# All broadcasts of the group weights issued in one row; the last group's statistics split over two queues

## The chip, the core and the metric

The kernel runs on one core of one Trainium2 chip. The metric is the device time of one execution in microseconds, as the median of several runs. The engines named below are PE (TensorE, the matrix products), DVE (VectorE), ACT (ScalarE), POOL (GpSimd) and SP (SyncE, which only issues transfers). Each engine works through its own instructions in program order and waits on semaphores for the others. ACT, POOL and SP can issue DMA transfers, each into a queue of its own; all queues run on the same 16 DMA engines.

## The reference

One layer of a decoder over 1024 tokens of width 1024, in three sub-layers:

- Sub-layer 1: `a = RMSNorm(x)`; one projection of `a` gives q, k, v of 12 attention heads (three groups of four heads with dilations 1, 4 and 16), a spatial-gating branch, and two sigmoid gates. Attention of each group `g` yields an output `o_g` and a log-denominator `lse_g` per head and token. Per head slot, `y = sum over g of softmax_g(lse_g) * o_g`. Then `merged = gate0 * (y @ w_branch_attn) + gate1 * (y_sgu @ w_branch_sgu)` and `h = x + merged @ w_out`.
- Sub-layer 2: RMSNorm, cross-attention into 256 memory tokens, residual.
- Sub-layer 3: RMSNorm, SwiGLU feed-forward, residual, and a last RMSNorm.

The change touches only the softmax over the three groups: its weights are computed from a maximum and a denominator per head and token, and multiplied onto the attention outputs.

## The kernel before

Everything is float32, each product made of three float32r products (high by high, high by low, low by high), so an operand exists as a pair: `wh`/`wl` for weights, `yAh`/`yAl` for the combined attention output. The large projections use a Strassen-Winograd scheme (lines 383 to 426). The work of sub-layer 1 is staged: projections, then spatial gating, then the product with `w_branch_sgu` (`branch_sgu`, PSUM tiles `psb`, 16 tiles of 12 matmuls), then the product with `w_branch_attn` (`branch_attn`, PSUM tiles `psa`, 16 tiles of 6 matmuls), then the output projection (`seven`, line 1165, PSUM tiles `psx` and `psy`). PSUM has eight banks, handed out in turn (`pp`, line 110); the pool for larger SBUF tiles (`heap`) has 20 buffers.

Attention runs as small pieces that are threaded in between the products of the other branches. The class `Order` (line 37) walks through the main program and lets a piece go on when its time in the plan has come; the tile framework then orders each engine's instructions and sets the waits. What follows the attention of a group is one such piece, `stats(g)`: PE turns the columns of maxima (`nmx`) and denominators (`den`) into rows, DVE copies them to `stT` (line 970), a transfer writes them to DRAM (`sc_d`, line 974, one for each `w_`: 0 is the maxima, 1 the denominators), and four loads for each `w_`, one per head (line 977), bring them back in the layout of `comb`, with 16 partitions per head (`stat`). POOL copies both parts into `comb` (line 981).

When the three groups are through, the piece `combine` works out the weights in `comb` (lines 988 to 999: DVE with one Exp on ACT), writes them to DRAM (`wt_d`, line 1000), and then, for each pair of heads `pr` and each group `g`, loads a tile `wbc` (line 1006): each head's row of 1024 weights is broadcast to 64 partitions, the first head of the pair by ACT's queue and the second by POOL's, 256 KB each. DVE multiplies `oT[g, pr]` by `wbc` (line 1007), adds the groups (lines 1008, 1009) and splits the sum into `yAh` (by ACT, line 137) and `yAl` (by DVE, line 140). `branch_attn` needs the `yAh` and `yAl` of both pairs for each of its tiles. In the kernel before, the loads of a pair stand in the program directly ahead of that pair's products.

While this goes on, PE works on `branch_sgu`, and DVE evacuates each `psb` tile by a product with `mg` (line 1033). On POOL's queue, behind the broadcasts, come the loads of the gates `sig` (line 1041, 512 KB each), which take buffers that the combination frees, and then the loads of `h` (line 1207). DVE evacuates `psa` with a product with `sig` (line 1050) and adds the result to `mg` (line 1051).

Of the kernel before, what the change touches and what calls it, by code (L numbers as in the profile page):

```python
# [15 lines left out]
P = 128  # L16
# [69 lines left out]
def tile_hybrid_dilated_attn_sgu_gated_block(  # L86
# [25 lines left out]
    nc = tc.nc  # L112
# [11 lines left out]
    def H(name, dt=F32, shape=(P, 1024)):  # L124
        return heap.tile(list(shape), dt, name=name, tag="h")
# [4 lines left out]
    def W(name, dt=F32, shape=(P, 512)):  # L130
        return wk.tile(list(shape), dt, name=name, tag="w")

    def PS(name="ps", shape=(P, 512)):
        return pp.tile(list(shape), F32, name=name, tag="p")

    def split(src, hi, lo, pin=False, eng=None):
        i = nc.scalar.activation(hi, src, AF.Copy)  # L137
        if pin:
            tc.keep_in_program_order(i)
        (eng or nc.vector).tensor_sub(lo, src, hi.bitcast(F32))  # L140
# [530 lines left out]
    qk, vts, oT = {}, {}, {}  # L671
# [170 lines left out]
    def spawn_attn():  # L842
        its = [(g, pr) for g in range(GROUPS) for pr in range(2)]

        def add(i):
            if i < len(its):
                load_qk(*its[i])
            yield 0.0, 0.0

        for i, (g, pr) in enumerate(its):  # L850
            st = {"n": 0}
            for n, it in enumerate(units(g)):
                order.spawn(attn_it(g, pr, it, st), delay=2.0, key="attn%d" % g)
                if n == 4:
                    order.spawn(add(i + 2), key="load")
            if pr == 1:
                order.spawn(stats(g), key="stats")
        order.spawn(combine(), key="combine")
# [96 lines left out]
    sc_d = dram.tile([GROUPS, 2, HPG, S], F32, name="sc_d")  # L955
    wt_d = dram.tile([GROUPS, HPG, S], F32, name="wt_d")

    def comb(i):
        return consts_["comb"][:64, i * 64:(i + 1) * 64]

    def stats(g):
        while order.busy("attn%d" % g):
            yield 0.0, 1.0
        if g == 0:
            consts_["comb"] = H("comb")
        ps = PS("pst")
        stT = W("stT")
        for w_, t in enumerate((nmx, den)):
            nc.tensor.transpose(ps[:32, w_ * P:(w_ + 1) * P], t[:, g * 32:(g + 1) * 32], ident)
        nc.vector.tensor_copy(stT[:32, :256], ps[:32, :256])  # L970
        d = DIL[g]
        stat = W("stat")
        for w_ in range(2):
            nc.sync.dma_start(sc_d[g, w_].rearrange("h (b q) -> (h b) q", q=P), stT[:32, w_ * P:(w_ + 1) * P])
            src = sc_d[g, w_].rearrange("h (r c i) -> h c r i", r=d, i=64 // d)
            for h in range(HPG):
                nc.sync.dma_start(
                    stat[h * 16:(h + 1) * 16, w_ * 64:(w_ + 1) * 64].rearrange("p (r i) -> p r i", r=d), src[h])
        yield 0.22, 0.0
        for w_ in range(2):  # L980
            nc.gpsimd.tensor_copy(comb(3 * w_ + g).rearrange("p (i r) -> p i r", r=d),
                                  stat[:64, w_ * 64:(w_ + 1) * 64].rearrange("p (r i) -> p i r", r=d))

    def combine():
        while order.busy("stats"):
            yield 0.0, 1.0
        low, tot = comb(6), comb(7)
        nc.vector.tensor_tensor(low, comb(0), comb(1), op=ALU.min)
        nc.vector.tensor_tensor(low, low, comb(2), op=ALU.min)
        for g in range(3):  # L990
            nc.vector.tensor_sub(comb(g), low, comb(g))
        n_, dn_ = [consts_["comb"][:64, i * 192:(i + 1) * 192] for i in range(2)]
        nc.scalar.activation(n_, n_, AF.Exp)
        nc.vector.tensor_mul(dn_, dn_, n_)
        nc.vector.tensor_add(tot, comb(3), comb(4))
        nc.vector.tensor_add(tot, tot, comb(5))
        nc.vector.reciprocal(low, tot)
        for g in range(3):
            nc.vector.tensor_mul(comb(g), comb(g), low)
            nc.scalar.dma_start(wt_d[g].rearrange("h (c i) -> (h c) i", i=64), comb(g))  # L1000
        for pr in range(2):
            for g in range(3):
                t = H("wbc")
                for hh in range(2):
                    src = wt_d[g, 2 * pr + hh:2 * pr + hh + 1, :]
                    (nc.scalar, nc.gpsimd)[hh].dma_start(t[hh * HD:(hh + 1) * HD, :], src.to_broadcast([HD, S]))
                nc.vector.tensor_mul(oT[g, pr], oT[g, pr], t)
            nc.vector.tensor_add(oT[0, pr], oT[0, pr], oT[1, pr])
            nc.vector.tensor_add(oT[0, pr], oT[0, pr], oT[2, pr])
            y = H("yAh", F32R), H("yAl", F32R)  # L1010
            split(oT[0, pr], *y)
            yA.append(y)
            yield 0.0, 0.0
# [82 lines left out]
    h = []  # L1096
# [24 lines left out]
    WPART = ("W11", "W21", "T2", "T1", "W22", "T3", "T4")  # L1121

    def seven(kp, raw, weights, combine, done, tail, after=None, todo=()):


# [4 lines left out]
        def prep(n):  # L1130
            s_, k = steps[n]
            if k % 2 == 0:
                wld[s_] = load([weights[WPART[s_]][k:min(k + 2, kp)].rearrange("k p c -> p k c")])[0]
            hi = whl.tile([P, 1024], F32R, name="wh", tag="hi")
            lo = whl.tile([P, 1024], F32R, name="wl", tag="lo")
            split(raw(s_, k), hi[:, :HALF], lo[:, :HALF])
            split(wld[s_][:, (k % 2) * HALF:(k % 2 + 1) * HALF], hi[:, HALF:], lo[:, HALF:])
            ready[n] = (hi, lo)
            combine(s_, k)
# [507 lines left out]
```

## Time and profile before

| what | value |
|---|---|
| median of 3 runs | 1486.52 us (1485.70 to 1486.54) |
| the profiled execution's own time | 1485.01 us |
| its span | 1483.2 us |
| PE busy | 1445.8 us (97%) |
| DVE busy | 993.5 us (67%) |
| ACT busy | 609.2 us (41%) |
| POOL busy | 143.4 us (10%) |

The span is what the profiler saw between the first and the last instruction; the execution's own time is 1.8 us longer. PE is busy nearly throughout, so what can be changed in the time is to be looked for in the few places in which PE has nothing to do, or runs at the lower clock. A busy PE says nothing of its pace; the granted clock of a stretch (1.00 is 2.4 GHz, 0.50 is 1.2 GHz) and the distance from one matmul's start to the next do.

### The profile page before, as it was taken

To read this page: it belongs to the slowest core of one execution; us is meant where nothing else is said; L and a number is where in the kernel's file an instruction comes from. 1 tells how busy PE (TensorE), PEld (TensorE's weight loads), DVE (VectorE), ACT (ScalarE), POOL (GpSimd) and SP (SyncE) were. 2 spreads that over 40 slices of the span, in tenths; PEclk is the share of its full clock that TensorE was granted. 3 is DMA by queue.
4 is the path that set the end of the run, shared out by engine and by line. 5 is a ranking of instruction groups with operands and counts; after the bars stand their busy time and mean duration, and the time that the engine had idled before them with its cause. 6 is when DMAs were issued, how large, how long until landed. Compare 5 with 4: busy or idle time off the path is not lost.

```text
span 1483.2 us, 19504 instructions
## 1 busy us (share of the span) xinstructions
PE 1445.8 (97%) x7375; PEld 1210.7 (82%) x7375; DVE 993.5 (67%) x1855; ACT 609.2 (41%) x1150; POOL 143.4 (10%) x166
## 2 busy tenths in 40 slices
PE   8999999999998999899999999999999999999997
PEld 8899888888887768687888888888888888888876
DVE  7786555555546855898677896666666663876596
ACT  4245233343335771135456752222222221454463
POOL 5300000000012112100000000110110002200030
PEclk9999999999999999999999999999999999999999
DMA  6224333793379247532211313885874225943342
GB/s 214 65 91 129 115 114 114 208 244 108 108 237 311 85 173 185 161 115 68 72 53 62 114 58 119 213 209 143 219 176 129 80 84 184 377 149 93 107 149 78
DMA packets 162897, 211.78 MB, mean 143 GB/s; under 512 B 9150, under 2 KB 110258, under 8 KB 162676
## 3 DMA queue, kind: packets, MB, share of 16 engines
q1 hardware_dynamic: 134304, 127.09, 27.1%
q0 software_dynamic: 22640, 68.98, 16.8%
q10 hardware_dynamic: 5860, 14.47, 3.0%
q8 instruction: 58, 0.95, 0.3%
q14 instruction: 35, 0.29, 0.1%
HBM read 168.43 MB, written 73.55 MB: 163 GB/s over the span
## 4 chain that ended last, share of the span: by engine, by line
PE 84%; DVE 7%; DMA 5%; ACT 2%; issue 1%; POOL 0%; SPq 0%; ACTq 0%; POOLq 0%; DVEq 0%
PE psb L390 20%; PE psc L390 13%; PE psg L390 13%; PE psx L1165 8%; PE psy L1165 8%; PE psv L170 1%; PE psv L169 1%; PE psv L171 1%; DVE wl L140 1%; DMA wbc<-wt_d 1%; PE psb L469 1%; PE psq L171 1%; PE psq L170 1%; PE psq L169 1%; DVE nq L204 1%
## 5 line engine op out<-in xcount | busy, mean ns | idle before, releaser
L137 ACT ACTIVATE wh<-wst 128x1024 fp32r<-128x1024 f32 (+1 forms) x213 | 178.7, 840 | 348.2 <-PE psg L390 244.3
L140 DVE TENSOR_TENSOR wl<-wst,wh 128x512 fp32r<-128x512 f32 (+1 forms) x209 | 205.1, 983 | 82.2 <-ACT wh L137 82.2
L390 PE MATMUL psg<-A,wh 128*128 128x512 f32 x592 | 182.5, 389 | 0.0
L390 PEld LDWEIGHTS psg<-A,wh 128*128 128x128 f32 x592 | 111.1, 188 | 22.9
L390 PE MATMUL psg<-A,wl 128*128 128x512 f32 x296 | 115.2, 389 | 0.0
L390 PE MATMUL psc<-S,t 128*128 128x512 f32 x444 | 106.6, 389 | 0.0
L390 PEld LDWEIGHTS psc<-S,t 128*128 128x128 f32 x444 | 83.4, 188 | 17.3
L1165 PE MATMUL psx<-wh 128*128 128x512 f32 x240 | 93.9, 393 | 3.1 <-DVE h L1177 3.1
L1165 PE MATMUL psx<-wl,wh 128*128 128x512 f32 x240 | 94.4, 393 | 0.6 <-DVE wl L140 0.6
L1165 PE MATMUL psx<-wh,wl 128*128 128x512 f32 x240 | 94.0, 393 | 0.0
L390 PE MATMUL psc<-S,wh 128*128 128x512 f32 x296 | 91.4, 390 | 0.0
L390 PE MATMUL psb<-S,wh 128*128 128x512 f32 x296 | 91.3, 390 | 0.0
L390 PE MATMUL psb<-S,t2h 128*128 128x512 f32 x296 | 91.2, 389 | 0.0
L140 DVE TENSOR_TENSOR wl<-hm,wh 128x512 fp32r<-128x512 f32 x77 | 55.9, 726 | 50.3 <-ACT wh L137 50.2
L390 PE MATMUL psb<-A,t2h 128*128 128x512 f32 x288 | 88.8, 390 | 0.6 <-DVE v L1423 0.6
L137 ACT ACTIVATE wh<-hm 128x512 fp32r<-128x512 f32 x77 | 48.4, 630 | 95.0 <-PE psy L1165 45.8
L411 DVE TENSOR_TENSOR u<-p,psb 128x512 f32<-128x512 f32 x37 | 25.4, 687 | 90.1 <-PE psb L390 90.1
L1165 PE MATMUL psy<-wh 128*128 128x512 f32 x180 | 70.2, 390 | 0.3 <-ACT wh L137 0.3
L1165 PE MATMUL psy<-wh,wl 128*128 128x512 f32 x180 | 70.1, 389 | 0.0
L1165 PE MATMUL psy<-wl,wh 128*128 128x512 f32 x180 | 70.1, 389 | 0.0
L414 DVE TENSOR_TENSOR v<-p,psc 128x512 f32<-128x512 f32 x37 | 25.4, 687 | 64.8 <-PE psc L390 64.8
L390 PEld LDWEIGHTS psg<-A,wl 128*128 128x128 f32 x296 | 55.6, 188 | 11.6
(354 smaller groups left out, 3395.8 us busy)
## 6 DMA issues: line engine op xcount, KB each, us to landing
wst<-in_w_gate_up_dram SPq DMA_DIRECT2D x44, 512.0 KB, 4.9
wst<-in_w_in_dram SPq DMA_DIRECT2D x42, 512.0 KB, 4.9
hm_d<-hmf SPq DMA_DIRECT2D x44, 256.0 KB, 4.4
hm<-hm_d POOLq DMA_DIRECT2D x22, 512.0 KB, 9.3
wst<-wdT SPq DMA_DIRECT2D x20, 512.0 KB, 3.7
wdT<-in_w_down_dram POOLq DMA_DIRECT2D x12, 768.0 KB, 9.1
sig_d<-act ACTq DMA_DIRECT2D x16, 512.0 KB, 3.7
wst<-in_w_down_dram SPq DMA_DIRECT2D x15, 512.0 KB, 5.4
```

The lines of the kernel that those rows point to most:

```text
L137: i = nc.scalar.activation(hi, src, AF.Copy)
L140: (eng or nc.vector).tensor_sub(lo, src, hi.bitcast(F32))
L169: nc.tensor.matmul(ps, lhsT=lh, rhs=rh, start=(i == 0), stop=False)
L170: nc.tensor.matmul(ps, lhsT=lh, rhs=rl, start=False, stop=False)
L171: nc.tensor.matmul(ps, lhsT=ll, rhs=rh, start=False, stop=(i == n - 1))
L204: nc.vector.scalar_tensor_tensor(q[:, c:c + 1], y[:, c:c + 1], ms[i][:, c:c + 1], y[:, c:c + 1], op0=ALU.mult, op1=ALU.mult)
L390: nc.tensor.matmul(ps, lhsT=l, rhs=r, start=first and k == 0 and i == 0, stop=k == 3 and i == 2, skip_group_check=not first)
L411: nc.vector.tensor_add(u, p1, b)
L414: nc.vector.tensor_add(v, p1, c)
L469: nc.tensor.matmul(p, lhsT=l, rhs=r, start=first and t % 2 == 0 and k == 0 and i == 0, stop=k == 3 and i == 2, skip_group_check=not first ...
L1165: nc.tensor.matmul(bank[t], lhsT=l, rhs=r, start=fresh and i == 0, stop=k == kp - 1 and i == 2, skip_group_check=s_ not in (0, 1, 3))
```

## The change

Two edits. In `stats`, the last group (`g` = 2) no longer uses SP's queue: its maxima go out and come back by ACT's queue, its denominators by POOL's. In `combine`, all twelve broadcasts are issued in one loop, ahead of the first product.

```diff
@@ -971,10 +971,11 @@
         d = DIL[g]
         stat = W("stat")
         for w_ in range(2):
-            nc.sync.dma_start(sc_d[g, w_].rearrange("h (b q) -> (h b) q", q=P), stT[:32, w_ * P:(w_ + 1) * P])
+            q = nc.sync if g < 2 else (nc.scalar, nc.gpsimd)[w_]
+            q.dma_start(sc_d[g, w_].rearrange("h (b q) -> (h b) q", q=P), stT[:32, w_ * P:(w_ + 1) * P])
             src = sc_d[g, w_].rearrange("h (r c i) -> h c r i", r=d, i=64 // d)
             for h in range(HPG):
-                nc.sync.dma_start(
+                q.dma_start(
                     stat[h * 16:(h + 1) * 16, w_ * 64:(w_ + 1) * 64].rearrange("p (r i) -> p r i", r=d), src[h])
         yield 0.22, 0.0
         for w_ in range(2):
@@ -998,13 +999,16 @@
         for g in range(3):
             nc.vector.tensor_mul(comb(g), comb(g), low)
             nc.scalar.dma_start(wt_d[g].rearrange("h (c i) -> (h c) i", i=64), comb(g))
+        wbc = {}
         for pr in range(2):
             for g in range(3):
-                t = H("wbc")
+                t = wbc[g, pr] = H("wbc")
                 for hh in range(2):
                     src = wt_d[g, 2 * pr + hh:2 * pr + hh + 1, :]
                     (nc.scalar, nc.gpsimd)[hh].dma_start(t[hh * HD:(hh + 1) * HD, :], src.to_broadcast([HD, S]))
-                nc.vector.tensor_mul(oT[g, pr], oT[g, pr], t)
+        for pr in range(2):
+            for g in range(3):
+                nc.vector.tensor_mul(oT[g, pr], oT[g, pr], wbc[g, pr])
             nc.vector.tensor_add(oT[0, pr], oT[0, pr], oT[1, pr])
             nc.vector.tensor_add(oT[0, pr], oT[0, pr], oT[2, pr])
             y = H("yAh", F32R), H("yAl", F32R)
```

On ACT, from the end of the attention to the second split of `yA`, the instructions stood in this order before (line numbers are those of each kernel's own file; from line 972 on those of the changed one are 1 to 4 higher):

```order
L839 ACTIVATE oT<-psO 128x4x128 x2
L137 ACTIVATE wh<-wst 128x1024
L993 ACTIVATE comb<-comb 64x192
L1000 DMA wt_d<-comb 64x64 x3
L1006 DMA wbc<-wt_d 64x1024 x3
L137 ACTIVATE wh<-wst 128x1024
L137 ACTIVATE yAh<-oT 128x1024
L1006 DMA wbc<-wt_d 64x1024 x3
L137 ACTIVATE wh<-wst 128x512
L137 ACTIVATE yAh<-oT 128x1024
```

and now they stand in this one:

```order
L839 ACTIVATE oT<-psO 128x4x128 x2
L975 DMA sc_d<-stT 32x128
L978 DMA stat<-sc_d 16x8x8 x4
L137 ACTIVATE wh<-wst 128x1024
L994 ACTIVATE comb<-comb 64x192
L1001 DMA wt_d<-comb 64x64 x3
L1008 DMA wbc<-wt_d 64x1024 x6
L137 ACTIVATE wh<-wst 128x1024
L137 ACTIVATE yAh<-oT 128x1024
L137 ACTIVATE wh<-wst 128x512
L137 ACTIVATE yAh<-oT 128x1024
```

The second pair's three broadcasts moved from behind the first pair's `yAh` to directly behind the first three, and the store and four loads of the last group's maxima came in ahead of a weight split.

On POOL, the rows between the last `mg` loads and the `sig` loads now read as follows; before, the four copies stood together and no `sc_d` or `stat` row was there, and the six broadcasts already stood together:

```order
L1026 DMA mg<-sig_d 128x2x512 x8
L982 COPY comb<-stat 64x64 x2
L975 DMA sc_d<-stT 32x128
L978 DMA stat<-sc_d 16x8x8 x4
L982 COPY comb<-stat 64x64 x2
L1008 DMA wbc<-wt_d 64x1024 x6
L1045 DMA sig<-sig_d 128x2x512 x8
```

So POOL's store and four loads of the denominators stand ahead of both copies of the last group. SP's queue lost two stores and eight loads at this place, and nothing came in for them.

On DVE, in the changed kernel, the stretch from the third product with `wbc` on stands as below (numbers tell the tiles apart: `oT_4010`, `oT_4397`, `oT_4801` are the first pair, `oT_4172`, `oT_4614`, `oT_4936` the second; `psb_5246` to `psb_5274` are the second to fourth tile of the third step of `branch_sgu`):

```order
L1011 TENSOR_TENSOR oT_4801<-oT_4801,wbc_5104 128x1024
L1012 TENSOR_TENSOR oT_4010<-oT_4010,oT_4397 128x1024
L1011 TENSOR_TENSOR oT_4172<-oT_4172,wbc_5107 128x1024
L1013 TENSOR_TENSOR oT_4010<-oT_4010,oT_4801 128x1024
L1011 TENSOR_TENSOR oT_4614<-oT_4614,wbc_5110 128x1024
L1011 TENSOR_TENSOR oT_4936<-oT_4936,wbc_5113 128x1024
L140 TENSOR_TENSOR yAl_5122<-oT_4010,yAh_5121 128x1024
L1012 TENSOR_TENSOR oT_4172<-oT_4172,oT_4614 128x1024
L1037 TENSOR_TENSOR mg_5229<-mg_5229,psb_5246 128x512
L1013 TENSOR_TENSOR oT_4172<-oT_4172,oT_4936 128x1024
L1037 TENSOR_TENSOR mg_5229<-mg_5229,psb_5260 128x512
L1037 TENSOR_TENSOR mg_5229<-mg_5229,psb_5274 128x512
```

Before, the three evacuations of `psb_5246`, `psb_5260` and `psb_5274` stood ahead of the second pair's first product; now they stand behind all three of them. The second pair's `yAl` follows directly behind the last of these rows, and behind it four more `mg` products and two weight splits (`wl`), one of them 128x1024 wide, which stood earlier before. PE's order is the same up to the last stage: the same matmuls, with a few of `psa` and of `psx`/`psy` no longer exchanged among each other.

## Rows read from the trace of the kernel before

**Rows 1.** Waits of PE over the whole span: us in total, times, longest

```profile
PE psa L169 <- ACT yAh L137: 6.2, 1, 6.2
```

**Rows 2.** Timeline of PE: start, us, line, count, idle before and its releaser

```profile
559.96 0.39 PE L171 MATMUL psb<-yS,wl 128*128 128x512 f32 x1
...
594.19 0.39 PE L169 MATMUL psa<-yAh,wh 128*128 128x512 f32 x1
...
601.26 1.22 PE L169 MATMUL psa<-yAh,wh 128*128 128x512 f32 x2 [6.23 <-ACT yAh L137]
...
624.78 0.39 PE L1165 MATMUL psx<-wh 128*128 128x512 f32 x1
...
628.90 0.50 PE L1165 MATMUL psy<-wh 128*128 128x512 f32 x1 [0.34 <-ACT wh L137]
```

**Rows 3.** Busy time by window: length, PE, PEld, DVE, ACT, POOL, clock, DMA share, GB/s

```profile
595.00:600.00 5.00, 0.03 (x1) 0.00 (x0) 4.92 (x6) 0.00 (x0) 1.81 (x3) 0.93 0.74 231
600.00:605.00 5.00, 3.74 (x9) 2.97 (x10) 2.46 (x4) 1.06 (x1) 1.06 (x2) 0.50 0.95 315
605.00:610.00 5.00, 5.00 (x21) 4.04 (x20) 3.88 (x5) 1.67 (x3) 0.53 (x1) 0.88 0.39 113
```

**Rows 4.** Timeline of ACT and its queue

```profile
569.02 1.82 ACTq L1006 DMA_DIRECT2D wbc<-wt_d  x3
...
582.55 2.02 ACTq L1006 DMA_DIRECT2D wbc<-wt_d  x3
...
600.15 1.06 ACT L137 ACTIVATE yAh<-oT 128x1024 fp32r<-128x1024 f32 x1 [14.90 <-DVE oT L1009]
```

**Rows 5.** Timeline of DVE

```profile
578.36 1.22 DVE L1007 TENSOR_TENSOR oT<-oT,wbc 128x1024 f32<-128x1024 f32 x1 [0.49 <-DMA wbc<-wt_d]
579.50 1.22 DVE L1008 TENSOR_TENSOR oT<-oT 128x1024 f32<-128x1024 f32 x1
580.64 0.68 DVE L1033 TENSOR_TENSOR mg<-mg,psb 128x512 f32<-128x512 f32 x1
581.23 1.22 DVE L1009 TENSOR_TENSOR oT<-oT 128x1024 f32<-128x1024 f32 x1
...
591.44 1.22 DVE L1007 TENSOR_TENSOR oT<-oT,wbc 128x1024 f32<-128x1024 f32 x1 [5.52 <-DMA wbc<-wt_d]
```

**Rows 6.** Timeline of SP's queue

```profile
557.44 0.78 SPq L974 DMA_DIRECT2D sc_d<-stT  x2
559.89 3.63 SPq L977 DMA_DIRECT2D stat<-sc_d  x8
```

**Rows 7.** Timeline of POOL and its queue

```profile
562.96 1.05 POOL L981 COPY comb<-stat 64x64 f32<-64x64 f32 x1 [18.50 <-DMA stat<-sc_d]
564.80 0.29 POOL L981 COPY comb<-stat 64x64 f32<-64x64 f32 x1 [0.79 <-DMA stat<-sc_d]
569.41 3.32 POOL L1006 DMA_DIRECT2D wbc<-wt_d  x6 [4.31 <-DMA wt_d<-comb]
```

**Rows 8.** Tile stat: time from issue to landing of its 24 loads

```profile
DMA to landing us min/median/max: 1.5/1.6/3.2
```

**Rows 9.** DMA queues from 566 to 571: packets, MB, share (q10 is ACT's)

```profile
q10 hardware_dynamic: 277, 0.20, 18.2%
```

**Rows 10.** DMA queues from 571 to 574 (q0 is POOL's)

```profile
q0 software_dynamic: 112, 0.39, 52.4%
q10 hardware_dynamic: 120, 0.37, 51.1%
```

**Rows 11.** DMA queues from 577 to 580

```profile
q0 software_dynamic: 191, 0.63, 105.7%
```

**Rows 12.** DMA queues from 586 to 589

```profile
q10 hardware_dynamic: 103, 0.36, 51.4%
```

**Rows 13.** Tile rowc (six loads by POOL, 2 to 8 KB, at the start): issue to landing

```profile
DMA to landing us min/median/max: 5.4/5.7/6.1
```

**Rows 14.** Tile wbc (twelve loads by ACT and POOL): issue to landing

```profile
DMA to landing us min/median/max: 3.6/7.6/12.2
```

## The prediction, made before the changed kernel was run

> **What bounds the kernel now.** I read the waits of PE first, since PE is busy 97% of the span. The longest single wait is at the start of `branch_attn`: a `psa` matmul waits 6.2 us for `yAh` [rows 1]. The timeline of PE shows it in place [rows 2]: the first `psa` matmul starts at 594.19, three run, then 6.23 us of nothing until 601.26. The price is larger than the wait. Over the psb stretch, 151 matmul starts lie between 559.96 and 594.19, so one takes 34.23 / 151 = 0.2267 us. `branch_attn` has 16 tiles of 6 = 96 matmuls, which at that pace take 21.76 us; they took 624.78 - 594.19 = 30.59 [rows 2]. So 8.83 us are lost there: 6.23 in the wait, some 0.16 in draining and refilling, and 2.43 in pace. The pace shows in the granted clock: 0.50 (1.2 GHz) from 600 to 605, after PE had been idle since 595, and 0.88 on average from 605 to 610 [rows 3]. A second wait of 0.34 us follows at 628.90 for a `wh` [rows 2], since DVE and ACT come late there too.
>
> Why is `yAh` late? I followed it back. ACT splits it at 600.15, as soon as DVE has the sum [rows 4]. DVE's first product of the second pair starts at 591.44, after 5.52 us of waiting for `wbc` [rows 5]. Three of the second pair's six broadcasts were issued by ACT at 582.55 only [rows 4], behind the first pair's `yAh` in ACT's queue; the first pair's were issued from 569.02, and POOL issued all six of its own from 569.41 on without a break [rows 4, 7]. So POOL's half of the second pair was long there, and ACT's half was late twice: 13.5 us in issue, then behind the `sig` loads. That half began to move only about 586, when ACT's queue is seen again with 0.36 MB in 3 us [rows 12].
>
> **Part one: the broadcasts in a row.** Nothing is added in bytes or instructions. ACT issues three transfers in 1.82 us [rows 4], so six take 3.6: 569.0 to 572.7. What stands behind them on ACT, a weight split, then runs at 572.7, and the first `yAh` isn't due before 583. So the issue costs nothing.
>
> When do the second pair's tiles land? From 571 to 574 both queues moved 0.39 + 0.37 = 0.76 MB, 0.25 per us, in equal shares [rows 10]. From 577 to 580 POOL's queue alone, with its second-pair halves, moved 0.63, 0.21 per us [rows 11]. The engines are full with broadcasts either way. A tile is 512 KB = 0.524 MB, so 2.1 to 2.5 us each; I take 2.3. The third tile of the first pair was there at 578.36 [rows 5]. With each queue working in order, the first pair keeps its times, and the next three land 2.3 us apart: 580.7, 583.0, 585.3. The `sig` loads stand behind POOL's broadcasts, as before.
>
> Now DVE, in its new order, from rows 5: a 128x1024 instruction starts 1.14 us after the one before (578.36 to 579.50), a 128x512 one takes 0.59. I shift all by 0.5 for part two (below). Third product 578.9 to 580.0; sum to 581.2; first product of the second pair (landed 581.2) to 582.3; sum to 583.5; second product (landed 583.5) to 584.6; third (landed 585.8) to 586.9; first `yAl` to 588.1; sum to 589.2; `psb_5246` to 589.8; last sum to 590.9. ACT's split takes 1.06 [rows 4], so the second `yAh` is there at 592.0. DVE does two evacuations to 592.1 and the second `yAl` to 593.2. PE wants `yAh` with the fourth `psa` matmul, at 594.19 + 3 x 0.2267 = 594.87, and `yAl` at 595.10. So the wait goes, with about 1.9 us in hand, and with it the fall of the clock: 8.83 us.
>
> What covers this? The second pair's products now stand ahead of three evacuations of `psb`, so PE must not run out of PSUM. `psb_5246` is emptied at 589.8. With eight banks in turn, its bank is wanted again by the eighth tile after it, the second of `psa`, at 594.19 + 6 x 0.2267 = 595.55. That holds by 5.7 us; the cover would be gone if the last broadcast landed that much later.
>
> What is late next? DVE, which by its new order has four `mg` products and two weight splits between `yAl` and the first `sig` product: 4 x 0.59 + 1.14 + 0.59 = 4.1, so to 597.3; the first `psa` tile is done near 595.7. So DVE starts 1.6 us behind. In each step of two tiles it needs 2 x 0.59 + 1.14 = 2.32 against PE's 12 x 0.2267 = 2.72, so it gains 0.4 per step, 3.2 over eight, and pays five splits of 0.6 that its new order puts there: it ends about as far behind as it began, and eight banks of 1.36 us cover 10 us. The 0.34 at 628.90 should go too, since DVE is then no later against PE than before. Total of part one: 9.2 at most.
>
> **Part two: the statistics by ACT and POOL.** On SP, the first store is issued at 557.44, the loads from 559.89, eight of them in 3.63 us, 0.45 each [rows 6]; a load lands 1.6 after its issue [rows 8]. POOL copied the maxima at 562.96 and the denominators at 564.80 [rows 7]. Now ACT: store 557.5, loads from 559.9, four at 0.6 (from rows 4) to 562.3, landed 563.3: 0.3 later than before. The weight split that ran ahead on ACT now runs at 562.3 and holds DVE's part of it, ahead of the first `comb` step, to 564.6 against 564.05 before: 0.5 late. POOL: its transfers show no byte before 571 although the first was issued at 569.41, while ACT's, issued at 569.02, move before that [rows 7, 9, 10]. I put that at 0.5 us per landing, twice: loads from 560.4, four at 3.32 / 6 = 0.55, last issued 562.1, landed 564.2, which is 0.6 earlier than before. The maxima are then the later ones, and the chain starts 0.5 late. Bounds: with POOL as quick as SP and no split in ACT's way, 1.6 early; with the 5.7 us of the small `rowc` loads [rows 13], which ran beside full queues, twice, 557.5 + 5.7 + 1.65 + 5.7 = 570.5, 5.7 late. I take 0.5 late: at this place the engines move almost nothing, so the row of `stat` is nearer than that of `rowc`. It costs nothing as long as the 1.9 us in hand last.
>
> The eight loads took 3.63 us to issue where one lands in 1.6 [rows 6, 8], so the issue was the larger part. The Trainium skill ("DMA: Bandwidth & Descriptors", "Issuing engines are not separate DMA queues") says that starting transfers on several engines saves only the sequencer's time, usually small beside the transfer. By it the split is worth at most half of the issue, 1.8 us, and here the trace has that as the larger share. The same page ("Latency and other measured facts") gives a first byte after about 0.6 us on the hardware queues and about 1 us on GpSimd's, which speaks against the split; as an estimate from it, twice 0.4 = 0.8 us would be given back on the denominators. The trace agrees in direction, no more.
>
> **The sum.** I take 9.0: 8.83, and half of the 0.34. In the profiled execution's own time, 1485.01 - 9.0 = 1476.0. The median of the runs stands 1.5 above that execution, so 1477.5.
>
> **The rivals.** Let L be the time to landing of POOL's small transfers, so the denominators come at 557.5 + 2L + 1.65, against 564.8.
>
> *Late, but not fully.* With L = 5.7 the chain is 5.7 late instead of 0.5; the second `yAl` comes at 598.4, PE waits 3.3, and loses up to 2.4 in pace again: gain 3.3, 1483.2. With 3.5 late, 1.1 + up to 2.4: 1481. For it: rows 13, and only 1.9 us in hand. Against: those loads ran under load.
>
> *No change, since the broadcasts share instead of queueing.* If all twelve move side by side, none lands before 585.8, and DVE has six products, four sums, two `yAl` and five evacuations to do from there: 12 x 1.14 + 5 x 0.59 = 16.6, second `yAl` at 602.4, PE waits 7.3 and loses the pace: 9.7 against 8.8 now, 1487.4. For it: one row for everything, as the change issues it. Against: before, three plus six were under way together, and the first three tiles came by 578.36 at the shared rate, in order [rows 5, 10].
>
> *Slower: POOL's queue holds the statistics up.* The same place as the first rival, but decided by L. PE is worse off by over 3 us when the second `yAl` comes after 604.4, that is 11.7 us late, L = 8.8. The `wbc` loads had a median of 7.6 and a longest of 12.2 [rows 14]; at L = 10 the chain is 14.4 late, `yAl` at 607.1, the loss 12.0 + 2.4, and the time 1492. Against: those were 256 KB behind others on full engines, these are 4 to 16 KB on idle ones.
>
> **How the numbers follow.** Forecast 0.74, own range 1476 to 1479.5; late 0.14; no change 0.07; slower 0.05. What a measurement here can tell from no change is 0.2%, 3.0 us. Faster takes the first two, 0.86 with a little off the edge of the second; same 0.09; slower 0.05. The range reaches from 1475.5 to 1483.5. The upper end is that of the late case. The lower one is the full 9.2 (1477.3) and 1.8 for what I can't price: the 0.8 by which the runs differ, and a us in the later stages.
>
> **What would show it.** ACT's six broadcasts within 4 us near 569.5; the last `wbc` landed by 586.5; DVE's sixth product ended by 587.5; no wait of PE at `psa` and a clock of 1.00 from 590 to 610; the first `psx` matmul at 616, not 624.8. Part two is right if POOL's second copy starts within 1 us of 564.8 and `wt_d` is issued near 567.5. I am wrong if POOL's copies start after 566.7, if the first pair's third product starts well after 579, or if PE waits at a `psb` tile for its bank.

## The result, and the profile after

The changed kernel takes 1476.42 us (median of 4 runs, 1474.38 to 1477.30), the kernel before 1486.53 (4 runs, 1485.70 to 1488.67). The ratio is 0.9928 [0.9911, 0.9945]: faster by 0.72%, or 10.1 us. Forecast were 1477.5 in a range of 1475.5 to 1483.5, and faster with 0.86. The profiled execution of the changed kernel took 1477.30, with a span of 1475.5, against 1485.01 and 1483.2.

Where the time came from shows at the place that the prediction named. The waits of PE come first: the costliest row of the whole span is now the one below. The list's top of before, the 6.2 us at `psa` [rows 1], is gone, and no `psa` and no `psy` stands in the list any more.

```profile
PE psT L596 <- DVE hn L584: 3.2, 1, 3.2
```

PE's timeline after: the transpose that begins the change's stretch (`pst`, which feeds DVE's copy into `stT`), the first two `psa` matmuls, and the first `psx`, which follows the last `psa`.

```profile
558.07 0.28 PE L969 MATMUL pst<-ident,nmx 128*32 128x128 f32 x1
...
595.75 0.39 PE L169 MATMUL psa<-yAh,wh 128*128 128x512 f32 x1
595.98 0.39 PE L170 MATMUL psa<-yAl,wh 128*128 128x512 f32 x1
...
617.51 0.39 PE L1169 MATMUL psx<-wh 128*128 128x512 f32 x1
```

From the first `psa` to the first `psx` it is 617.51 - 595.75 = 21.76 us, that is 0.2267 for each of the 96 matmuls, the pace of the stage in front. Before it was 30.59 [rows 2]. So 8.83 us went here, and no idle stands at 628.90's counterpart: the 0.34 went too. The windows (length, busy PE, PEld, DVE, ACT, POOL, granted clock, DMA share, GB/s) show the clock that stood at 0.93, 0.50 and 0.88 [rows 3]:

```profile
595.00:600.00 5.00, 5.00 (x24) 4.14 (x23) 4.96 (x8) 0.00 (x0) 0.00 (x0) 1.00 1.02 404
600.00:605.00 5.00, 5.00 (x23) 4.14 (x23) 4.90 (x8) 1.68 (x3) 0.76 (x2) 1.00 0.77 268
605.00:610.00 5.00, 5.00 (x23) 4.14 (x23) 5.00 (x8) 0.00 (x0) 0.82 (x2) 1.00 0.51 149
```

ACT's queue shows why. Its six broadcasts (L1008) now leave in one row, where three of them waited for 582.55 before [rows 4]. The second `yAh` is split at 591.84, not 600.15; counted from the copy into `stT`, at 33.27 us, not 43.15.

```profile
561.44 1.78 ACTq L978 DMA_DIRECT2D stat<-sc_d  x4
563.27 1.06 ACT L137 ACTIVATE wh<-wst 128x1024 fp32r<-128x1024 f32 x1 [3.88 <-DMA stat<-sc_d]
...
568.92 1.81 ACTq L1001 DMA_DIRECT2D wt_d<-comb  x3
570.85 3.80 ACTq L1008 DMA_DIRECT2D wbc<-wt_d  x6
...
591.84 1.06 ACT L137 ACTIVATE yAh<-oT 128x1024 fp32r<-128x1024 f32 x1 [4.69 <-DVE oT L1013]
```

DVE's timeline (a weight split `wl` and the first `comb` step come first; they are read further down): the first pair's third product waits 0.76 for its tile; the second pair's three products (583.18, then two from 585.46) wait for nothing. In [rows 5] the first of them waited 5.52 us and started at 591.44.

```profile
558.57 0.41 DVE L970 COPY stT<-pst 32x256 f32<-32x256 f32 x1 [2.59 <-PE pst L969]
...
564.36 1.23 DVE L140 TENSOR_TENSOR wl<-wst,wh 128x1024 fp32r<-128x1024 f32 x1 [0.36 <-ACT wh L137]
565.78 0.31 DVE L990 TENSOR_TENSOR comb<-comb 64x64 f32<-64x64 f32 x1 [0.19 <-POOL comb L982]
...
580.90 1.23 DVE L1011 TENSOR_TENSOR oT<-oT,wbc 128x1024 f32<-128x1024 f32 x1 [0.76 <-DMA wbc<-wt_d]
...
583.18 1.22 DVE L1011 TENSOR_TENSOR oT<-oT,wbc 128x1024 f32<-128x1024 f32 x1
...
585.46 2.35 DVE L1011 TENSOR_TENSOR oT<-oT,wbc 128x1024 f32<-128x1024 f32 x2
...
592.94 1.23 DVE L140 TENSOR_TENSOR yAl<-oT,yAh 128x1024 fp32r<-128x1024 f32 x1
...
598.21 1.27 DVE L1054 TENSOR_TENSOR sig<-sig,psa 128x512 f32<-128x512 f32 x2
```

The two queues from 580 to 583 (packets, MB, share; q10 is ACT's, q0 POOL's): equal shares, 0.92 MB in 3 us. POOL's queue no longer runs ahead alone [rows 11].

```profile
q10 hardware_dynamic: 136, 0.46, 52.3%
q0 software_dynamic: 134, 0.46, 51.7%
```

Last, POOL with its half of the statistics: its two copies into `comb` now follow each other.

```profile
559.27 0.54 POOL L975 DMA_DIRECT2D sc_d<-stT  x1 [14.12 <-DVE stT L970]
562.10 2.11 POOL L978 DMA_DIRECT2D stat<-sc_d  x4 [2.28 <-issue]
564.79 1.22 POOL L982 COPY comb<-stat 64x64 f32<-64x64 f32 x2 [0.58 <-DMA stat<-sc_d]
```

### The profile page after: what moved, and what is told of

Read it like the earlier page. It is cut to its first block, busy times and chain, and to the rows that moved or that the text cites. A ratio compares the mean times of both kernels' runs of the same rounds, so it can differ in the third digit from the quotient of the medians.

```text
span 1475.5 us, 19494 instructions
## 1 busy us (share of the span) xinstructions
PE 1447.4 (98%) x7375; PEld 1210.9 (82%) x7375; DVE 992.6 (67%) x1855; ACT 609.2 (41%) x1150; POOL 146.2 (10%) x171
## 4 chain that ended last, share of the span: by engine, by line
PE 86%; DVE 6%; DMA 4%; ACT 2%; issue 1%; POOL 0%; SPq 0%; ACTq 0%; DVEq 0%; POOLq 0%
PE psb L390 19%; PE psc L390 13%; PE psg L390 13%; PE psx L1169 9%; PE psy L1169 8%; DMA wst<-in_w_in_dram 2%; DVE wl L140 1%; PE psv L169 1%; PE psv L170 1%; PE psv L171 1%; PE psb L469 1%; PE psb L169 1%; PE psb L170 1%; PE psq L171 1%; PE psq L169 1%; PE psb L171 1%
```

## The experiments

One caution holds for all of them. The stage in front of the change is the same code, yet in the eight profiled executions `stT` was copied anywhere from 556.7 to 563.6 us. So two traces are compared by distances within each: from `pst` to the first `psx`, and from the start of the `stT` copy to the issue of `wt_d` (the end of the statistics chain).

| kernel | median us (runs) | ratio to before | first `psa` | first `psx` | `pst` to `psx` | `stT` to `wt_d` |
|---|---|---|---|---|---|---|
| before (first comparison) | 1486.53 (4) | 1 | 594.19 | 624.78 | 68.28 | 10.09 |
| after | 1476.42 (4) | 0.9928 [0.9911, 0.9945] | 595.75 | 617.51 | 59.44 | 10.35 |
| row only | 1477.56 (6) | 0.9945 [0.9928, 0.9962] | 593.92 | 615.68 | 59.44 | 10.23 |
| split only | 1485.74 (12) | 0.9996 [0.9983, 1.0009] | 595.11 | 626.34 | 68.92 | 10.49 |
| halves by SP | 1480.22 (6) | 0.9957 [0.9942, 0.9973] | 599.35 | 623.89 | 62.23 | 10.07 |
| wait filled | 1483.99 (12) | 0.9988 [0.9976, 1.0000] | 606.92 | 630.38 | 67.26 | 10.08 |
| chain held, 4 | 1478.78 (10) | 0.9957 [0.9945, 0.9969] | 598.48 | 622.29 | 61.49 | 14.54 |
| chain held, 10 | 1490.68 (7) | 1.0041 [1.0027, 1.0055] | 598.87 | 629.68 | 72.57 | 20.84 |

The first four experiments shared 24 runs of before (1486.03), the last two 16 (1484.73), on another chip. The four kernels whose statistics go by SP stand between 10.07 and 10.23 in the last column, so a difference of 0.2 there says little.

**The row alone.** The changed kernel with the last group's statistics back on SP:

```
-            q = nc.sync if g < 2 else (nc.scalar, nc.gpsimd)[w_]
+            q = nc.sync
```

> The twelve broadcasts in one row, the last group's statistics on SP's queue as before. Theory (the row is the whole gain, the split only moves the chain by a few tenths and is hidden by the time in hand): within 0.1% of the changed kernel, ratio to before 0.993 to 0.995; no wait of PE at psa; wt_d is issued no later after the stT copy than in the changed kernel (9.7 us against 9.9). Rival (the earlier statistics carry part of the gain): 2 us or more slower than the changed kernel, with a wait at psa.

Measured: 0.9945, and `pst` to `psx` 59.44, to the hundredth that of the full change. Part one is the whole local gain. The times of the two versions, 1477.56 and 1476.42, have ratios whose intervals overlap. DVE's timeline shows what the split does to the time in hand: here the first pair's third product starts 578.14 - 556.74 = 21.40 us after the `stT` copy, as it did before (21.36), and the second `yAl` 33.43 after it; in the full change these are 22.33 and 34.37.

```profile
578.14 1.22 DVE L1011 TENSOR_TENSOR oT<-oT,wbc 128x1024 f32<-128x1024 f32 x1
...
590.17 1.23 DVE L140 TENSOR_TENSOR yAl<-oT,yAh 128x1024 fp32r<-128x1024 f32 x1
```

**The split alone.** The kernel before, with its own order of broadcasts, and the queues of part two:

```
-            nc.sync.dma_start(sc_d[g, w_]...
+            q = nc.sync if g < 2 else (nc.scalar, nc.gpsimd)[w_]
+            q.dma_start(sc_d[g, w_]...
...
-                nc.sync.dma_start(
+                q.dma_start(
```

> The statistics of the last group split over ACT and POOL, the broadcasts as before. Theory: no change, ratio 0.999 to 1.001, the wait at psa stays at 6 us or a few tenths more. Rival (the split shortens the chain by half of its issue, 1.8 us): 1.5 to 2 us faster, the wait at psa 4.4 us.

Measured: 0.9996 [0.9983, 1.0009], no change, with `wt_d` 0.40 us later in the chain. The wait of PE is still there, in the list of its waits, and 1.1 us longer than before, more than the few tenths expected:

```profile
PE psa L169 <- ACT yAh L137: 7.3, 1, 7.3
```

POOL's timeline in this run gives the two copies, 6.41 and 7.54 us behind the `stT` copy at 557.92, against 5.96 and 7.80 before [rows 7]: maxima later, denominators earlier.

```profile
564.33 0.95 POOL L982 COPY comb<-stat 64x64 f32<-64x64 f32 x1 [0.59 <-DMA stat<-sc_d]
565.46 0.29 POOL L982 COPY comb<-stat 64x64 f32<-64x64 f32 x1 [0.18 <-DMA stat<-sc_d]
```

By the first pair's third product the 0.40 had become 1.04: DVE starts it 580.32 - 557.92 = 22.40 us after the `stT` copy, and the second `yAh` comes 1.09 later than before.

```profile
580.32 1.23 DVE L1008 TENSOR_TENSOR oT<-oT,wbc 128x1024 f32<-128x1024 f32 x1 [0.83 <-DMA wbc<-wt_d]
```

**SP issues ACT's halves, as the products come.** The order of before, but another issuer:

```
-                    (nc.scalar, nc.gpsimd)[hh].dma_start(t[hh * HD:...
+                    (nc.sync, nc.gpsimd)[hh].dma_start(t[hh * HD:...
```

> The kernel before, only that the first halves of all broadcasts go by SP's queue instead of ACT's; they still stand pair by pair in the program. SP doesn't do arithmetic, so the second pair's halves no longer wait behind the first pair's yAh. Theory (they were late because they stood behind yAh on ACT): the wait at psa goes or falls under 2 us, 6 to 9 us faster, ratio 0.994 to 0.996. Rival (they were late because they came behind the sig loads on the DMA engines, whoever issues them): wait at psa of 4 us or more, at most 3 us faster.

Measured: 0.9957, which is 5.8 us in the medians, and 6.05 us better from `pst` to `psx`; that is at the lower edge of what the theory expected. SP's queue was free of `yAh`, but not free: the second pair's halves stood behind the weight load of 581.15.

```profile
581.15 0.39 SPq L147 DMA_DIRECT2D wst<-in_w_out_dram  x1
581.64 1.73 SPq L1006 DMA_DIRECT2D wbc<-wt_d  x3
```

They left 581.64 - 562.16 = 19.5 us after the `stT` copy, against 25.55 before and 14.2 for the fourth of ACT's row in the changed kernel. DVE's first product of the second pair then started 11.2 us after that issue (592.81, timeline of DVE), as it came 8.9 after it before [rows 4, 5].

```profile
592.81 1.23 DVE L1007 TENSOR_TENSOR oT<-oT,wbc 128x1024 f32<-128x1024 f32 x1 [2.34 <-DMA wbc<-wt_d]
```

So the first half of the cause is shown: with an issuer that doesn't stand behind the first pair's work, 6.05 of the 8.84 us come back. The second half, that late broadcasts move behind and among the `sig` loads, is read from the queues of the kernel before and not tested by itself (in this run the halves also stood behind SP's own weight load). Before, from 583 to 586, just after ACT's issue at 582.55, POOL's queue is the only one of the three that moves data, and ACT's shows no packet until 586 [rows 12]:

```profile
q0 software_dynamic: 309, 1.14, 100.6%
```

A better issuer alone leaves waits of 1.42 and 0.76 at `psa` (timeline of PE), with the clock at 1.00 through them (window).

```profile
601.60 0.50 PE L169 MATMUL psa<-yAh,wh 128*128 128x512 f32 x1 [1.42 <-ACT yAh L137]
...
602.86 0.50 PE L170 MATMUL psa<-yAl,wh 128*128 128x512 f32 x1 [0.76 <-DVE yAl L140]
```

```profile
600.00:605.00 5.00, 2.83 (x11) 1.96 (x11) 3.57 (x5) 1.06 (x1) 1.06 (x2) 1.00 1.02 395
```

**The wait filled.** The kernel before, with 27 products that nothing reads put on PE ahead of `branch_attn`, so that PE works where it waited:

```
         order.join("combine")
+        fill = PS("fill")
+        for n in range(27):
+            tc.keep_in_program_order(nc.tensor.matmul(fill, lhsT=yS[0][0][:, :P],
+                rhs=yS[0][0][:, :HALF], start=n == 0, stop=n == 26))
         yield from branch_attn()
```

> The kernel before, with 27 more 128x512 matmuls on PE between branch_sgu and branch_attn, whose result nothing reads (27 x 0.2267 = 6.1 us, the length of the wait). Theory (2.4 us of the 8.8 are the lower clock after the idle time): the clock stays at 1.00 from 595 to 610, the first psx matmul comes 2.2 to 2.6 us earlier than before, ratio 0.998 to 0.9985. Rival (the slow pace is the restart of the stage, DVE and the late halves of yA, not the clock): no change, or slower by the part of the 6.1 us that does not fit into the wait.

Measured: 0.9988 [0.9976, 1.0000]; 1.02 us better from `pst` to `psx`. The clock did as the theory says, 1.00 in both windows:

```profile
605.00:610.00 5.00, 3.89 (x17) 2.67 (x16) 4.32 (x6) 1.06 (x1) 2.01 (x4) 1.00 0.89 314
610.00:615.00 5.00, 5.00 (x24) 4.12 (x23) 4.02 (x6) 1.48 (x3) 0.67 (x2) 1.00 0.53 179
```

The gain is smaller than the 2.2 to 2.6 expected, and the timeline of PE says why:

```profile
608.12 0.51 PE L169 MATMUL psa<-yAh,wh 128*128 128x512 f32 x1 [0.36 <-ACT yAh L137]
...
609.38 0.51 PE L170 MATMUL psa<-yAl,wh 128*128 128x512 f32 x1 [0.76 <-DVE yAl L140]
...
630.38 0.39 PE L1165 MATMUL psx<-wh 128*128 128x512 f32 x1
```

Of the 96 matmuls 93 follow the wait: 93 x 0.2267 = 21.08 us. Before they took 624.78 - 601.26 = 23.52, so 2.44 was lost to the pace [rows 2]. Here they took 630.38 - 608.12 = 22.26: 1.18 is lost, with the clock full, of which 0.76 is a new wait for `yAl`. The first of them also stood 0.24 later behind `pst`. So 2.44 - 1.18 - 0.24 = 1.02. The new wait goes with PE's order, which changed with the fill. Before, two products with a `yAh` follow the wait [rows 2], and the next one with a `yAl` starts at 602.27, ahead of the end of the second `yAl` (601.24 + 1.22 = 602.46), so it belongs to another tile; here PE goes tile by tile and wants the second `yAl` with its next matmul. So the slow pace was real, 2.44 - 0.42 = 2.0 of it came back with the clock, and half of that was paid out again in the new wait and the 0.24.

**The chain held back.** The changed kernel, where POOL writes `stat` ahead of its loads for the last group (4 or 10 additions of about 1.1 us); the loads overwrite it, so the output stays as it was:

```
         stat = W("stat")
+        if g == 2:
+            nc.gpsimd.memset(stat, 0.0)
+            nc.gpsimd.tensor_copy(stat[:32, :256], stT[:32, :256])
+            for _ in range(4):      # 10 in the second kernel
+                nc.gpsimd.tensor_add(stat, stat, stat)
```

> The changed kernel with the last group's loads held back: POOL fills and doubles the tile stat first (a fill, a copy and four adds of 128x512, overwritten by the loads where it is used). The loads start some 4 us later. Theory (2.6 us in hand in the changed kernel, beyond them each us of delay is a us of PE waiting, and the clock falls on top): wait at psa of 1 to 2.5 us, time 1 to 4.5 us above the changed kernel. Rival (the broadcasts, not the statistics, set the end of the combination): time as that of the changed kernel.

Measured with 4: `wt_d` 4.19 us later than in the changed kernel, the second `yAl` 4.34 later (38.71 us after the `stT` copy, against 34.37), `psx` 2.05 later. PE waits twice, 1.47 us in all, as expected; but the clock doesn't fall, the granted clock of 600 to 605 is still 1.00 (timelines of PE and of DVE, then the window):

```profile
600.03 0.51 PE L169 MATMUL psa<-yAh,wh 128*128 128x512 f32 x1 [0.71 <-ACT yAh L137]
...
601.29 0.50 PE L170 MATMUL psa<-yAl,wh 128*128 128x512 f32 x1 [0.76 <-DVE yAl L140]
```

```profile
600.01 1.23 DVE L140 TENSOR_TENSOR yAl<-oT,yAh 128x1024 fp32r<-128x1024 f32 x1
```

```profile
600.00:605.00 5.00, 4.21 (x17) 3.27 (x18) 5.00 (x8) 0.00 (x0) 0.53 (x1) 1.00 1.03 398
```

> As e5_hold4 with ten adds: the loads start some 12 to 13 us later. Theory: wait at psa of 9 to 11 us and the lower clock behind it, 2 to 5 us slower than before (ratio 1.001 to 1.003), which is the point of the third rival of the prediction. Rival: less than half of the delay arrives at PE, since the broadcasts then meet emptier engines; faster than before by 3 us or more.

Measured with 10: `wt_d` 10.49 later, `psx` 13.13 later than in the changed kernel and 4.29 later than in the kernel before; in the runs 1.0041 [1.0027, 1.0055], slower by 6 us, more than the 2 to 5 expected. The delay grew on its way to PE. The tile framework ordered ACT's work otherwise in this kernel, with one weight split ahead of ACT's four loads and the next ahead of the broadcasts; the six broadcasts took 6.16 us to leave where they took 3.80 in the changed kernel, five of POOL's waited for `wt_d` a second time, and the second `yAl` came 605.80 - 557.61 = 48.19 us after the `stT` copy, 13.82 later than in the changed kernel (timelines of ACT's queue, POOL and DVE):

```profile
580.41 6.16 ACTq L1013 DMA_DIRECT2D wbc<-wt_d  x6
```

```profile
582.96 2.54 POOL L1013 DMA_DIRECT2D wbc<-wt_d  x5 [1.65 <-DMA wt_d<-comb]
```

```profile
605.80 1.23 DVE L140 TENSOR_TENSOR yAl<-oT,yAh 128x1024 fp32r<-128x1024 f32 x1
```

PE now waits for both pairs, and the clock falls (timeline of PE, then the windows):

```profile
598.87 0.79 PE L169 MATMUL psa<-yAh,wh 128*128 128x512 f32 x1 [3.92 <-ACT yAh L137]
...
601.87 0.79 PE L170 MATMUL psa<-yAl,wh 128*128 128x512 f32 x1 [2.21 <-DVE yAl L140]
...
605.82 0.79 PE L169 MATMUL psa<-yAh,wh 128*128 128x512 f32 x1 [2.73 <-ACT yAh L137]
...
607.08 0.79 PE L170 MATMUL psa<-yAl,wh 128*128 128x512 f32 x1 [0.47 <-DVE yAl L140]
```

```profile
595.00:600.00 5.00, 0.79 (x1) 0.29 (x1) 4.04 (x4) 1.06 (x1) 2.43 (x4) 0.69 1.04 298
600.00:605.00 5.00, 1.22 (x2) 0.50 (x2) 5.00 (x6) 0.29 (x1) 2.28 (x5) 0.50 1.02 384
605.00:610.00 5.00, 3.71 (x8) 2.63 (x9) 5.00 (x8) 0.77 (x1) 1.03 (x2) 0.50 1.03 392
```

This is the prediction's third rival made to happen: with its statistics held up on POOL, and with what that did to ACT's order and to the row of broadcasts, the kernel is slower than before.

## Why the prediction was right, step by step

**The wait and its clock, 8.83 us.** Measured 8.84 from `pst` to `psx`, in the full change and with the row alone. The terms are shown one by one: the wait is gone from the list, the clock is 1.00 through the stretch, and the filled wait shows that the fall of the clock came from PE's idling, not from what ran beside it. The 0.34 at `psy` went as well, so the local sum is 9.2, the upper value named. The sum itself had taken half of the 0.34.

**The second pair's landing.** Forecast was one tile each 2.3 us, with DVE waiting for each. The queues did share equally, in order, and the first pair keeps its times under the row, as forecast: its third product started 21.40 us after the `stT` copy with the row alone, against 21.36 before [rows 5]. The 22.33 of the full change belongs to part two (below). None of the next three products waited: DVE itself was the pace. That the broadcasts would share instead of queueing, the "no change" rival, is refuted by this.

**The time in hand.** Forecast 1.9 us, measured more. The second `yAl` starts at 592.94 and takes 1.23, so it is there at 594.17; PE wants it with its fifth `psa` matmul, at 595.75 + 4 x 0.2267 = 596.66. That is 2.5 in hand. With the row alone it is there at 591.40 and wanted at 594.83: 3.4 in hand. So part two spent 0.9 of it. The chain held with four additions bears on the 2.5 from the other side: 4.34 late at `yAl`, less 2.5, leaves 1.8, and 2.05 was lost. The cover by PSUM held as well: PE waited at no `psb` tile in this stretch.

**Part two, 0.5 late.** Its mechanism was right as far as `wt_d`; its size was too large there and too small behind it. From the `stT` copy, DVE's first `comb` step stood at 7.05 before, 7.21 in the changed kernel, 7.40 with the split alone; `wt_d` was issued 0.26 and 0.40 later. The reason is the weight split on ACT, which stands behind ACT's four loads and holds DVE's part of it, `wl`, which begins 5.62 us after the `stT` copy before, and 5.79 and 5.98 in these two. Before, in DVE's timeline:

```profile
562.62 1.23 DVE L140 TENSOR_TENSOR wl<-wst,wh 128x1024 fp32r<-128x1024 f32 x1 [0.18 <-ACT wh L137]
...
564.05 0.22 DVE L989 TENSOR_TENSOR comb<-comb 64x64 f32<-64x64 f32 x1 [0.20 <-POOL comb L981]
```

The trace names POOL's copy of the maxima as the one that releases the step. But that copy hung on `wl` too: beside `wl` it took 1.05 us before and 0.96 and 0.95 in these two, and ended about 0.15 after `wl`; with ten additions, where `wl` was long through, it took 0.29. POOL's copies were both done earlier than the later one before, as was forecast.

From `wt_d` to the products the delay grew, which the forecast didn't see: the first pair's third product stood at 21.36 before, 21.40 with the row alone and 21.67 with the wait filled, and at 22.33 and 22.40 in the two kernels with the split. So the split costs 0.7 to 1.0 us there, more than the 0.5. Why the broadcasts come later by more than `wt_d` isn't shown. In the full change this cost no time, because the time in hand covered it, as the forecast said.

So moving half of the loads off SP gained nothing in the end: what it took from SP's issue [rows 6] it put in front of something that the chain also waits for.

The Trainium skill ("DMA: Bandwidth & Descriptors", "Issuing engines are not separate DMA queues") allows a split over engines to save only the sequencer's time. The runs agree with that limit: 0.9996 alone, and no part of it reached the path.

**DVE behind at the first `sig` product.** Forecast 1.6 us behind PE; the first product started at 598.21, and the first `psa` tile was done near 595.75 + 6 x 0.2267 + 0.16 = 597.3, so 0.9. DVE was busy nearly all of the time from 595 to 610 (4.96, 4.90 and 5.00 of each 5 us) and PE never waited for it.

**The rivals.** "Late, but not fully" and "slower" were one mechanism, and the two held kernels put it on a scale: counted at the second `yAl`, as the prediction counts, 4.34 late costs 2.05 and 13.82 late costs 13.13. Its way of counting holds: 13.82 less the 2.5 in hand, and 2.4 of pace on top, make 13.7. It let the change cross into slower by over 3 us at 11.7 late; at 13.82 it was 4.29 slower in the trace and 6 in the runs. What it didn't see is that 10.49 at `wt_d` would become 13.82 at `yAl`. Of the 13.13 the waits are 3.92 + 2.21 + 2.73 + 0.47 = 9.33; the other 3.8 is mostly pace, for the clock lay low from the first place of waiting past the last. In the changed kernel POOL's small transfers were as quick as the forecast had taken them, so this didn't arise.

**The size.** Forecast 9.0; the medians differ by 10.1, the profiled executions by 7.7. Neither is the change's own figure: in the changed kernel's profiled execution the stage in front ended 558.07 - 556.50 = 1.57 later than in that of before, which explains the 7.7 (9.2 - 1.57 = 7.6). The 0.9 that the medians differ by beyond 9.2 lies within the interval of the ratio (8.2 to 13.2 us), and the row alone, with the same local gain, is 1486.03 - 1477.56 = 8.5 us faster in its runs. So no run shows a gain beyond 9.2, and that the median came out so near the lower end of the range, 1475.5, is best put down to the spread of the runs.

## What to carry to other kernels

A transfer that needs nothing new shouldn't stand in an engine's queue behind an instruction that waits for other work: here three loads, which could have followed the first three at 570.8, left at 582.55, when the loads that stood behind them were already on the engines. Price a wait of PE by the whole stretch up to where the pace is back, not by its idle time (8.83 against 6.23 here), and find out how much is in hand behind the fix, since the same mechanism turned the gain into a loss once the second `yAl` came 13.8 us late. Before splitting a row of loads over engines, look at what stands behind them on those engines: here the split took 0.9 us of the time in hand and gave none back.

## What the runs showed that was not expected

- The same code in front of the change ended up to 7 us apart in different executions (`stT` copy from 556.7 to 563.6), while the medians of before stayed within 2 us (1484.73 to 1486.53). Single runs spread as widely as that (before, 1483.18 to 1491.58), and the profiled execution of the filled kernel, with the 563.6, was 5.3 us above its median. A gain of some us is read by distances within a trace.
- Short waits left the clock alone: 1.42 and 0.76 us close together, and 0.71 and 0.76, stood in windows at 1.00. Waits of 6.2 us, and of 3.92 followed by 2.21, were followed by windows at 0.50.
- Three broadcasts issued late took 8.9 us (before) and 11.2 us (halves by SP) until the first product that needs them, among the `sig` loads; in a row ahead of them they cost DVE no wait at all.
